# Norm factors of a hybrid encoder layer: one product with ones, a root on ScalarE and a Newton step on VectorE in place of column sums, power and broadcast

## The chip, the cores and the metric

The kernel runs on one core of one Trainium2 chip. The metric is the device time in microseconds (us) of one execution, as the median of several runs. The engines are called as the profile calls them: PE is TensorE (its weight loads are PEld), DVE is VectorE, ACT is ScalarE, POOL is GpSimd, SP is SyncE, which here issues most of the loads.

## What is computed

One layer of a hybrid encoder is applied to 1024 prompt frames and 64 sample frames (1088 positions in all, 1024 channels). Every norm divides by the root of a mean square over channels:

```python
def rmsnorm(x, g):
    y = xf * lax.rsqrt(jnp.mean(xf * xf, axis=-1, keepdims=True) + EPS) * g

def layer(x, ...):
    hn = rmsnorm(x, g_pre1);  z = hn @ w_in            # gate_a | xa | u | v
    h = rg_lru(causal_dwconv(xa, ...), ...)
    ya = rmsnorm(h * gelu(gate_a), g_out_a)            # half 0 of the output norm
    yb = rmsnorm(spatial_gate(u, layernorm(v), w_s), g_out_b)   # half 1
    mix = concatenate([ya, yb]) @ w_o
    x = x + rmsnorm(mix, g_post1)                      # rr1 below
    up = rmsnorm(x, g_pre2) @ w_up                     # rr2 below
    f = (gelu(conv(up)[:D_FF]) * conv(up)[D_FF:]) @ w_down
    x = x + rmsnorm(f, g_post2)                        # finish below
```

EPS is 1e-6. The change concerns how `rsqrt(mean + EPS)`, the norm factor of each position, is made and brought to all 128 partitions.

## The kernel before

Channels lie on the 128 partitions and positions along the columns, so a sum over channels is a sum over partitions, which PE makes. `cs(c)` cuts the 1088 columns in three chunks (364, 364, 360), `qs(q)` in four quarters (274, 274, 274, 266). Matrix products are made from operands split in a high and a low part (`split`, L139 to L142: ACT rounds the high part, DVE subtracts for the low one), three products each.

A norm factor is made in two steps. `rstd_head` (L187) lets PE sum the squares: three blocks of up to 95 columns are loaded as weights and multiplied with a single column of ones (L193, six instructions, since an fp32 product is issued in two), so that the sums of a block stand on its partitions, in three columns. `rstd_small` scales and adds EPS on DVE (L184) and raises to the power -0.5 on POOL (L185). `rstd_tail` (L200) brings the factors to all partitions with three products of the broadcast factors with the identity (L205, six instructions) and copies the result out of PSUM on ACT (L209). There are 20 such factors:

- half 1 of the output norm, four quarters (`y_split(c, 1)`), stepped through while the gate tiles 0 to 2 run on PE (`gate_tile`, products L425, evacuation by DVE in L551, gelu on ACT L553, product with h L555). The normed rows are made on DVE in L605 and split in L607;
- half 0, four quarters (`y_split(c, 0)`);
- `post1` (L701), twice a quarter c: the post-norm (rr1, applied in L711, residual added in L712, stored in L716) and the pre-norm (rr2, applied in L737), then the split into the operands bh and bl and, after each second quarter, differences of operands (L750). While the quarters c = 2 and 3 go through this, PE already makes the first up-projection products of the quarters 0 to 2 (`pre_up`, L775, three quarters c in a row);
- `finish` for three column ranges (272, 272, 284) of the down-projection's output, applied in L1112 eight times each, beside the last products (L1067), whose weights DVE combines in L1007 and splits in L142;
- `finish_last` for the last 260 columns, at the end.

The Tile framework schedules: each engine executes its instructions in a fixed order, found from the order of the program and from priorities (`tc.high_priority(offset=PRI)` pulls instructions ahead). The pool `stp` has 2 PSUM buffers, which the sums, the broadcasts and the gates of the recurrence share; `mmp` has the other 6, so that two gate tiles of three chunks fill it. The order of SP's queue is that of the program: the store L716 stands ahead of the loads of w_up.

Of the kernel before, what the change touches and what calls it, by code (L numbers as in the profile page):

```python
# [14 lines left out]
P = 128  # L15
# [52 lines left out]
def layer_kernel(ctx: ExitStack, tc, xT, w_fm, w_v, w_o, w_up, w_down, w_g, w_s, par, bc, yT, small, vn_out):  # L68
# [14 lines left out]
    def big_tile(dt=F32, shape=(P, TW), name="t"):  # L83
        return big.tile(list(shape), dt, tag="t", name=name)

    def tmp_tile(w, name="d"):
        return tmp.tile([P, 288], F32, tag="d", name=name)[:, :w]
# [17 lines left out]
    def qs(q):  # L105
        return slice(q * QW, min(q * QW + QW, T))
# [28 lines left out]
    nc.gpsimd.memset(ones, 1.0)  # L135
    mhalf = const.tile([P, 16], F32, name="mhalf")
    sm = const.tile([P, NSMALL], F32, name="sm")

    def split(hi, lo, src, scale=None):  # L139
        nc.scalar.activation(hi, src, AF.Copy, scale=1.0 if scale is None else scale)  # L140
# [43 lines left out]
            nc.vector.tensor_scalar(v[:n[0], :n[1]], src, 1.0 / dim, EPS, op0=ALU.mult, op1=ALU.add)  # L184
            nc.gpsimd.tensor_tensor(out, v[:n[0], :n[1]], mhalf[:n[0], :n[1]], op=ALU.pow)  # L185

    def rstd_head(ssq, dim, more=None):  # L187
        w = ssq.shape[-1]
        sb = -(-w // NSB)
        st = stp.tile([P, 512], F32, tag="st", name="st")  # L190
        for b in range(NSB):
            o = min(b * sb, w - sb)
            nc.tensor.matmul(st[:sb, b:b + 1], ssq[:, o:o + sb], ones[:, 0:1], start=True, stop=more is None)  # L193
            if more is not None:
                nc.tensor.matmul(st[:sb, b:b + 1], more[:, o:o + sb], ones[:, 0:1], start=False, stop=True)
        rs = tiny.tile([P, 16], F32, tag="rs", name="rs")
        rstd_small(rs[:sb, :NSB], st[:sb, :NSB], (sb, NSB), dim)
        return rs, sb, w

    def rstd_tail(head, out):  # L200
        rs, sb, w = head
        bp = stp.tile([P, 512], F32, tag="st", name="bp")
        for b in range(NSB):
            lo, hi = b * sb, min(b * sb + sb, w)
            mm = nc.tensor.matmul(bp[:, lo:hi], rs[:sb, b:b + 1].to_broadcast([sb, P]), ident[:sb, lo + sb - hi:sb],  # L205
                                  start=True, stop=True)
            if b == 0:
                tc.keep_in_program_order(mm)
        nc.scalar.activation(out, bp[:, :w], AF.Copy)  # L209
        return bp[:, :w]  # L210

    def add_sq(acc, src, first, eng=None):
        if first:
# [379 lines left out]
    yh, yl = {}, {}  # L593

    def y_split(c, half):
        head = rstd_head((sat if half == 0 else sbt)[:, qs(c)], DA, None if half else sat3[c])
        yield
        w = qw(c)
        rr = tmp_tile(w, name="rr")
        rstd_tail(head, rr)  # L600
        th, tl = big_tile(F32R, name="yh"), big_tile(F32R, name="yl")
        for i in range(4):
            k = half * 4 + i
            y = (hst[i] if half == 0 else s[i])[:, qs(c)]
            nc.vector.scalar_tensor_tensor(y, y, pv("g_out", k), rr, op0=ALU.mult, op1=ALU.mult)  # L605
            yh[k, c], yl[k, c] = th[:, fourth(i, w)], tl[:, fourth(i, w)]
            split(yh[k, c], yl[k, c], y)  # L607
            if i == 1:
                yield
# [5 lines left out]
    def run(gen):  # L615
        for _ in gen:
            pass

    ys = [y_split(c, 1) for c in range(4)]

    def y_steps(n):
# [499 lines left out]

    def finish_last(cols, more):
        w = cols.stop - cols.start
        head = rstd_head(ssqt[0][:, cols], D, more)
        scale_f(3, cols)
        rr = tmp_tile(w, name="rrf")
        bp = rstd_tail(head, rr)
        for g, q in ((1, nc.sync), (0, nc.scalar)):
            for m in range(4):
                f = fg[g][:, m, :]  # L1130
                nc.vector.tensor_tensor(f, f, bp, op=ALU.mult)
            nc.gpsimd.dma_start(yT[:, 4 * g:4 * g + 4, cols], fg[g], accum_op=ALU.add)
# [145 lines left out]
```

## Time and profile before

| what | value |
|---|---|
| median of 3 runs | 1176.99 us (1176.88 to 1177.64) |
| profiled execution, its own time | 1176.07 us |
| its span | 1173.9 us |
| mean granted TensorE clock | 0.987 of full |
| busy share: PE, DVE, ACT, POOL | 96%, 72%, 46%, 15% |
| chain that ended last, by engine | PE 86%, issue 6%, DMA 3%, DVE 2%, POOL 1%, ACT 1% |

The span is what the profile's rows cover; the execution's own time is 2.2 us more, and the median of the runs 0.92 us above that. An engine's busy share is an average over the whole span: stages in which DVE is full stand beside others in which it waits. The chain is followed back from the last instruction, at each step to what released it. In a timeline, a row holds one or several like instructions, their start, the time from the first's start to the last's end, and in brackets the idle time ahead of it with what ended it.

### The profile page before, as it was taken

The page shows a single profiled execution, that of the slowest core. Times are in us where ns is not written, and L with a number is a line of the kernel's source. Part 1 is how long each engine was busy: PE and PEld are TensorE (multiplying, and loading weights), DVE is VectorE, ACT ScalarE, POOL GpSimd, SP SyncE. Part 2 cuts the span into 40 slices and gives each one's busy share as a digit, 9 for nine tenths or more (in the row PEclk, how much of TensorE's full clock was granted, in tenths as well). Part 3 has the DMA queues.
Part 4 walks back from the last instruction along what each step waited for, and adds up shares of the span by engine and source line. Part 5 has one row for each costly group of instructions (what it writes and reads, how often), then busy time and mean ns, then how long its engine had stood idle before and what let it go on. Part 6 is the DMA issues. An engine that isn't in the chain of part 4 may idle for free.

```text
span 1173.9 us, 20616 instructions
## 1 busy us (share of the span) xinstructions
PE 1132.0 (96%) x8420; PEld 1109.0 (94%) x8420; DVE 841.0 (72%) x1363; ACT 534.2 (46%) x876; POOL 172.0 (15%) x291
## 2 busy tenths in 40 slices
PE   6899999999998999999999999999999999999984
PEld 4689999999998999999999999999999999999984
DVE  4568585865678789877877787787789365855753
ACT  4521675645444464444444454454456432523331
POOL 1030001110001113220211111112013000001213
PEclk8999999999999999999999999999999999999987
DMA  9811111140224123221322332232256779555925
GB/s 316 211 54 42 36 37 36 37 129 1 78 96 166 41 79 130 103 103 57 129 99 74 107 114 85 80 130 81 69 207 232 282 256 338 180 213 179 274 31 77
DMA packets 51566, 146.38 MB, mean 125 GB/s; under 512 B 5520, under 2 KB 21392, under 8 KB 51376
## 3 DMA queue, kind: packets, MB, share of 16 engines
q1 hardware_dynamic: 35936, 110.66, 27.3%
q0 software_dynamic: 15312, 34.27, 10.4%
q8 instruction: 66, 1.08, 0.4%
q14 instruction: 28, 0.23, 0.1%
q10 hardware_dynamic: 224, 0.14, 0.0%
HBM read 109.34 MB, written 41.99 MB: 129 GB/s over the span
## 4 chain that ended last, share of the span: by engine, by line
PE 86%; issue 6%; DMA 3%; DVE 2%; POOL 1%; ACT 1%; SPq 0%; POOLq 0%; DVEq 0%; ACTq 0%
PE up L906 40%; PE dps L1067 16%; PE ps L425 12%; PE ops L650 7%; PE pps L775 4%; PE vps L290 2%; DMA xr<-in_xT_dram 1%; DMA wraw<-in_w_v_dram 1%; PE gps L511 1%; PE bp L205 1%; POOL out_dram L1113 1%; PE sp L382 1%; PE st L193 1%; DVE gl L142 1%; ACT whi L140 1%
## 5 line engine op out<-in xcount | busy, mean ns | idle before, releaser
L906 PE MATMUL up<-bh,wop 128*128 128x274 f32 x2464 | 472.3, 290 | 0.0
L906 PEld LDWEIGHTS up<-bh,wop 128*128 128x128 f32 x2464 | 389.1, 189 | 1.7 <-ACT uraw L920 0.9
L906 PE MATMUL up<-bl,wop 128*128 128x274 f32 x1232 | 356.4, 289 | 0.0
L906 PEld LDWEIGHTS up<-bl,wop 128*128 128x128 f32 x1232 | 233.4, 189 | 0.0
L1067 PE MATMUL dps<-gh,whi 128*128 128x272 f32 x576 | 119.7, 289 | 0.7 <-ACT whi L140 0.5
L1067 PE MATMUL dps<-gl,whi 128*128 128x272 f32 x576 | 119.6, 288 | 0.0
L1067 PE MATMUL dps<-gh,wlo 128*128 128x272 f32 x576 | 119.1, 288 | 0.1
L142 DVE TENSOR_TENSOR wlo<-wraw,whi 128x1024 fp32r<-128x1024 f32 x70 | 85.4, 1221 | 35.4 <-ACT whi L140 34.8
L140 ACT ACTIVATE whi<-wraw 128x1024 fp32r<-128x1024 f32 x70 | 73.4, 1055 | 73.8 <-DVE wraw L1007 56.9
L140 ACT ACTIVATE wop<-wsum 128x512 fp32r<-128x512 f32 x88 | 53.0, 626 | 107.7 <-DVE wsum L862 105.3
L920 ACT ACTIVATE uraw<-up 128x274 f32<-128x274 f32 x176 | 65.6, 389 | 64.2 <-PE up L906 63.9
L1067 PEld LDWEIGHTS dps<-gh,whi 128*128 128x128 f32 x576 | 90.3, 188 | 1.1 <-ACT whi L140 0.7
L1067 PEld LDWEIGHTS dps<-gh,wlo 128*128 128x128 f32 x576 | 90.2, 188 | 0.4 <-DVE wlo L142 0.3
L1067 PEld LDWEIGHTS dps<-gl,whi 128*128 128x128 f32 x576 | 90.6, 188 | 0.0
L806 DVE SCALAR_TENSOR_TENSOR yg<-uraw,pt,yg 128x1090 f32<-128x1090 f32 (+1 forms) x48 | 64.8, 1350 | 26.2 <-ACT yg L804 26.2
L925 DVE TENSOR_TENSOR uraw<-up,uraw 128x274 f32<-128x274 f32 x132 | 56.3, 438 | 33.5 <-PE up L906 30.6
L650 PE MATMUL ops<-yh,whi 128*128 128x274 f32 (+1 forms) x256 | 75.3, 294 | 0.0
L650 PE MATMUL ops<-yl,whi 128*128 128x274 f32 (+1 forms) x256 | 73.8, 288 | 0.0
L650 PE MATMUL ops<-yh,wlo 128*128 128x274 f32 (+1 forms) x256 | 73.8, 288 | 0.0
L425 PE MATMUL ps<-xh,whi 128*128 128x364 f32 (+3 forms) x296 | 69.5, 328 | 0.0
L806 DVE SCALAR_TENSOR_TENSOR yv<-uraw,pt,yv 128x1090 f32<-128x1090 f32 (+1 forms) x48 | 64.6, 1346 | 4.8 <-ACT yv L804 4.7
L425 PE MATMUL ps<-xh,wlo 128*128 128x364 f32 (+3 forms) x296 | 67.6, 324 | 0.0
(220 smaller groups left out, 2143.7 us busy)
## 6 DMA issues: line engine op xcount, KB each, us to landing
wraw<-in_w_up_dram SPq DMA_DIRECT2D x48, 512.0 KB, 4.1
graw<-bd SPq DMA_DIRECT2D x42, 544.0 KB, 6.4
wraw<-in_w_down_dram SPq DMA_DIRECT2D x42, 512.0 KB, 5.4
bd<-yg POOLq DMA_DIRECT2D x36, 272.0 KB, 3.4
wraw<-sd SPq DMA_DIRECT2D x18, 512.0 KB, 5.4
bd<-ta POOLq DMA_DIRECT2D x24, 272.0 KB, 3.2
bd<-tb POOLq DMA_DIRECT2D x24, 272.0 KB, 3.0
wraw<-in_w_fm_dram SPq DMA_DIRECT2D x12, 512.0 KB, 3.6
```

The costliest lines, as they stand in the source:

```text
L140: nc.scalar.activation(hi, src, AF.Copy, scale=1.0 if scale is None else scale)
L142: nc.vector.tensor_tensor(lo, src, hi.bitcast(F32), op=ALU.subtract)
L193: nc.tensor.matmul(st[:sb, b:b + 1], ssq[:, o:o + sb], ones[:, 0:1], start=True, stop=more is None)
L290: nc.tensor.matmul(ps[b][:vrows(b), :], a[:, vcols(b)], wt[:, o:o + 512], start=False, stop=(k == KD - 1 and q == 2))
L425: nc.tensor.matmul(ps[c], wt[:, k * P:(k + 1) * P], at[k][:, cols], start=(k == 0 and q == 0), stop=(k == KD - 1 and q == 2))
L650: nc.tensor.matmul(ps, wt[:, i * 256 + mi * P:i * 256 + (mi + 1) * P], a[k, c], start=(first and i == 0 and j == 0), stop=(last and i == 3 ...
L775: nc.tensor.matmul(ps, wt[:, k * P:(k + 1) * P], a[k, c], start=(k == 0 and j == 0), stop=(k == KD - 1 and j == 2))
L806: nc.vector.scalar_tensor_tensor(y[:, d:TG], x[:, :TG - d], tap(2 - d), y[:, d:TG], op0=ALU.mult, op1=ALU.add)
L906: nc.tensor.matmul(dst[c], wt[:, k * P:(k + 1) * P], at[:, fourth(k)], start=(start and k == 0 and q == 0), stop=(k == 3 and q == 2), skip ...
L920: nc.scalar.activation(dst[c], src[c], AF.Copy)
L925: nc.vector.tensor_tensor(dst[c], src[c], p[c], op=ALU.add)
L1067: nc.tensor.matmul(ps, wt[:, k * 256 + mi * P:k * 256 + (mi + 1) * P], at[:, o + a:o + b], start=(first and k == 0 and q == 0), stop=(last ...
```

## The change

Fourteen factors are made in a new way, in place of fifteen of the old. PE multiplies the squares with a 128x128 tile of ones (one fp32 product, two instructions over all columns), so that each partition gets every sum at once. ACT takes the root of mean + EPS from PSUM; DVE takes the reciprocal; three DVE instructions make one Newton step with the sum that still stands in PSUM. The power on POOL, the broadcast products and the copy on ACT are gone there. Half 1 of the output norm is made in three chunks instead of four quarters, all of them ahead of the gate tiles. Half 0 and `finish_last` keep the old way under new names.

```diff
+    epst = const.tile([P, 1], F32, name="epst")
+    nc.gpsimd.memset(epst, EPS)
...
-    def rstd_head(ssq, dim, more=None):
+    def pow_head(ssq, dim, more=None):
...
-    def rstd_tail(head, out):
+    def pow_tail(head, out):
...
+    def rstd_head(ssq, dim, more=None):
+        w = ssq.shape[-1]
+        st = stp.tile([P, 512], F32, tag="st", name="sts")[:, :w]
+        nc.tensor.matmul(st, ones, ssq, start=True, stop=more is None)
+        if more is not None:
+            nc.tensor.matmul(st, ones, more, start=False, stop=True)
+        return st, dim
+
+    def rstd_tail(head, out):
+        st, dim = head
+        w = st.shape[-1]
+        e = (big_tile(name="rse") if w > 288 else tmp_tile(w, name="rse"))[:, :w]
+        with tc.high_priority(offset=PRI):
+            nc.scalar.activation(e, st, AF.Sqrt, scale=1.0 / dim, bias=epst)
+            nc.vector.reciprocal(out, e)
+            nc.vector.scalar_tensor_tensor(e, st, EPS * dim, out, op0=ALU.add, op1=ALU.mult)
+            nc.vector.scalar_tensor_tensor(e, e, -0.5 / dim, out, op0=ALU.mult, op1=ALU.mult)
+            nc.vector.scalar_tensor_tensor(out, e, 1.5, out, op0=ALU.add, op1=ALU.mult)
...
     def y_split(c, half):
-        head = rstd_head((sat if half == 0 else sbt)[:, qs(c)], DA, None if half else sat3[c])
-        yield
         w = qw(c)
-        rr = tmp_tile(w, name="rr")
-        rstd_tail(head, rr)
+        if half == 0:
+            head = pow_head(sat[:, qs(c)], DA, sat3[c])
+            yield
+            rr = tmp_tile(w, name="rr")
+            pow_tail(head, rr)
+        else:
+            yield
+            rr = rrb[:, qs(c)]
...
+    rrb = big_tile(name="rrb")[:, :T]
+    for c in range(3):
+        rstd_tail(rstd_head(sbt[:, cs(c)], DA), rrb[:, cs(c)])
     ys = [y_split(c, 1) for c in range(4)]
...
     def finish_last(cols, more):
...
-        head = rstd_head(ssqt[0][:, cols], D, more)
+        head = pow_head(ssqt[0][:, cols], D, more)
...
-        bp = rstd_tail(head, rr)
+        bp = pow_tail(head, rr)
```

In the changed kernel the new instructions are PE's product in the new `rstd_head` (its output is `sts`), the root in L227, the reciprocal in L228 and the Newton step in L229 to L231. Of the lines before, L551 is L572 there, L605 is L630, L142 is L144, L218 is L239, L737 is L765, L1007 is L1035, L1076 is L1104 and L1112 is L1140.

The order of DVE at the first gate tile, before (m and h are the last tile of the recurrence, L532 and L533 its scan; s are the rows of half 1, yl their low parts, gt the gate tile that leaves PSUM):

```order
L525 SCALAR_TENSOR_TENSOR m<-m,r 128x1088
L605 SCALAR_TENSOR_TENSOR s<-s,pt,rr 128x274 x4
L530 TENSOR_TENSOR m<-m,ig 128x1088
L532 SCALAR_TENSOR_TENSOR h<-a,m 128x1024
L533 SCALAR_TENSOR_TENSOR h<-a,pt,m 128x64
L142 TENSOR_TENSOR wlo<-wraw,whi 128x1024
L142 TENSOR_TENSOR yl<-s,yh 128x274 x4
L551 TENSOR_TENSOR gt<-ps,rbt 128x364 x2
L551 TENSOR_TENSOR gt<-ps,rbt 128x360
```

The same place in the changed kernel, from the scan on (rrb is the factor of half 1, rse a scratch tile):

```order
L553 SCALAR_TENSOR_TENSOR h<-a,m 128x1024
L228 RECIPROCAL rrb<-rse 128x364 x2
L229 SCALAR_TENSOR_TENSOR rse<-sts,rrb 128x364 x2
L230 SCALAR_TENSOR_TENSOR rse<-rse,rrb 128x364 x2
L231 SCALAR_TENSOR_TENSOR rrb<-rse,rrb 128x364
L228 RECIPROCAL rrb<-rse 128x360
L231 SCALAR_TENSOR_TENSOR rrb<-rse,rrb 128x364
L229 SCALAR_TENSOR_TENSOR rse<-sts,rrb 128x360
L554 SCALAR_TENSOR_TENSOR h<-a,pt,m 128x64
L230 SCALAR_TENSOR_TENSOR rse<-rse,rrb 128x360
L144 TENSOR_TENSOR wlo<-wraw,whi 128x1024
L231 SCALAR_TENSOR_TENSOR rrb<-rse,rrb 128x360
```

Three reciprocals and nine further instructions now stand between the scan and the first row of half 1 (L630), and with it ahead of the evacuation of gate tile 0 (L572), which stands behind the first four rows. The third sum has no PSUM buffer of `stp` until the first L229 has read its own.

The order of DVE at the third quarter's pre-norm and the fourth's post-norm, before (rr_3607 is rr2 of c = 2; the sum for rr1 of c = 3 goes through L184):

```order
L218 TENSOR_TENSOR ssq_o<-ssq_o,sq 128x266 x2
L737 SCALAR_TENSOR_TENSOR mix<-xs,pt,rr_3607 128x274
L218 TENSOR_TENSOR ssq_o<-ssq_o,sq 128x266
L737 SCALAR_TENSOR_TENSOR mix<-xs,pt,rr_3607 128x274
L184 TENSOR_SCALAR v<-st 89x3
L737 SCALAR_TENSOR_TENSOR mix<-xs,pt,rr_3607 128x274 x6
```

The same place in the changed kernel (rr_3547 is rr2 of c = 2, rr_3628 is rr1 of c = 3):

```order
L228 RECIPROCAL rr_3547<-rse 128x274
L239 TENSOR_TENSOR ssq_o<-ssq_o,sq 128x266
L229 SCALAR_TENSOR_TENSOR rse<-sts,rr_3547 128x274
L230 SCALAR_TENSOR_TENSOR rse<-rse,rr_3547 128x274
L231 SCALAR_TENSOR_TENSOR rr_3547<-rse,rr_3547 128x274
L228 RECIPROCAL rr_3628<-rse 128x266
L765 SCALAR_TENSOR_TENSOR mix<-xs,pt,rr_3547 128x274
L229 SCALAR_TENSOR_TENSOR rse<-sts,rr_3628 128x266
L765 SCALAR_TENSOR_TENSOR mix<-xs,pt,rr_3547 128x274
L230 SCALAR_TENSOR_TENSOR rse<-rse,rr_3628 128x266
L765 SCALAR_TENSOR_TENSOR mix<-xs,pt,rr_3547 128x274
L231 SCALAR_TENSOR_TENSOR rr_3628<-rse,rr_3628 128x266
```

Four instructions stand ahead of the first row of c = 2 (L765), and the four of the next factor between its rows.

The order of DVE at the second of the three `finish` ranges, before (facc is the down-projection's output, wraw a weight that is combined for the next products):

```order
L1112 SCALAR_TENSOR_TENSOR facc<-facc,pt,rrf 128x272
L1076 TENSOR_TENSOR facc<-dps,facc 128x272 x3
L1007 TENSOR_TENSOR wraw<-wraw 128x1024
```

The same place in the changed kernel:

```order
L228 RECIPROCAL rrf<-rse 128x272
L1104 TENSOR_TENSOR facc<-dps,facc 128x272
L229 SCALAR_TENSOR_TENSOR rse<-sts,rrf 128x272
L1104 TENSOR_TENSOR facc<-dps,facc 128x272
L230 SCALAR_TENSOR_TENSOR rse<-rse,rrf 128x272
L1035 TENSOR_TENSOR wraw<-wraw 128x1024
L231 SCALAR_TENSOR_TENSOR rrf<-rse,rrf 128x272
```

The reciprocal and two instructions of the Newton step stand ahead of the combined weight (L1035), and all eight rows of L1140 come together behind it, ahead of the next combined weight.

## Rows read from the trace of the kernel before

**Rows 1.** Page, part 1: busy time, share of the span, instructions.

```profile
PE 1132.0 (96%) x8420; PEld 1109.0 (94%) x8420; DVE 841.0 (72%) x1363; ACT 534.2 (46%) x876; POOL 172.0 (15%) x291
```

**Rows 2.** Stretches: core and stretch, span, busy (instructions) by engine, PEclk, DMA, GB/s.

```profile
216.00:232.00 16.00, 16.00 (x106) 15.99 (x106) 14.11 (x33) 10.45 (x20) 1.89 (x2) 1.00 0.12 38
...
338.00:363.00 25.00, 24.88 (x204) 24.66 (x202) 25.00 (x45) 11.82 (x21) 2.07 (x2) 1.00 0.32 99
363.00:377.30 14.30, 11.41 (x89) 10.98 (x89) 10.07 (x19) 8.87 (x18) 1.92 (x3) 1.00 0.45 169
...
1109.00:1122.00 13.00, 7.55 (x50) 6.52 (x48) 11.88 (x20) 4.90 (x6) 6.19 (x7) 0.90 0.82 145
1122.00:1145.00 23.00, 22.83 (x163) 22.56 (x163) 11.95 (x17) 8.08 (x13) 0.00 (x0) 0.91 0.06 8
```

**Rows 3.** Timeline of PE beside the first gate tile: start, us, engine, line.

```profile
200.95 0.57 PE L193 MATMUL st<-ones,sbt 128*92 128x1 f32 x6
...
201.96 0.57 PE L193 MATMUL st<-ones,sbt 128*92 128x1 f32 x6
...
204.96 0.66 PE L425 MATMUL ps<-xh,wlo 128*128 128x364 f32 x3
205.45 0.80 PE L205 MATMUL bp<-ident,rs 92*128 92x92 f32 x6
...
206.62 0.50 PE L425 MATMUL ps<-xl,whi 128*128 128x364 f32 x2
```

**Rows 4.** Timeline of PE at an fp32 product over 512 columns.

```profile
63.09 1.13 PE L355 MATMUL wsum<-bw,ones 128*128 128x512 f32 x2
...
64.52 0.40 PE L290 MATMUL vps<-wlo,xh 128*128 128x512 f32 x1
64.75 0.40 PE L290 MATMUL vps<-whi,xh 128*128 128x512 f32 x1
```

**Rows 5.** Who waits for POOL's power, over the span: us, times.

```profile
  PE bp L205: 3.6, 4
```

**Rows 6.** L457, L458 and L184 on DVE: ns min/median/max, first and last start, forms.

```profile
L457 DVE RECIPROCAL d<-d x1: 178/178/178, 9.6 to 9.6; 128x4 f32<-128x4 f32 x1
...
L458 DVE TENSOR_TENSOR e<-e,d x1: 161/161/161, 9.8 to 9.8; 128x4 f32<-128x4 f32 x1
...
L184 DVE TENSOR_SCALAR v<-stt x2: 140/153/166, 63.2 to 63.3; 128x8 f32<-128x8 f32 x1, 64x1 f32<-64x1 f32 x1
```

**Rows 7.** Timelines of ACT and DVE at the gate tiles.

```profile
204.21 1.29 DVE L525 SCALAR_TENSOR_TENSOR m<-m,r 128x1088 f32<-128x1088 f32 x1 [1.49 <-ACT m L524]
...
206.71 1.28 ACT L526 ACT_TABLE_LOAD   x1
...
210.69 2.29 DVE L532 TENSOR_TENSOR_SCAN h<-a,m 128x1024 f32<-128x1024 f32 x1
...
237.35 0.98 DVE L551 TENSOR_TENSOR gt<-ps,rbt 128x364 f32<-128x364 f32 x2 [0.73 <-PE ps L425]
```

**Rows 8.** Timelines of SP, ACT and PE at the third and fourth quarter.

```profile
357.31 0.38 SPq L716 DMA_DIRECT2D out_dram<-xs  x1
...
363.39 1.06 ACT L140 ACTIVATE whi<-wraw 128x1024 fp32r<-128x1024 f32 x1 [4.69 <-DMA wraw<-in_w_up_dram]
...
363.87 0.90 PE L205 MATMUL bp<-ident,rs 92*128 92x92 f32 x6 [0.98 <-POOL rs L185]
...
377.31 0.52 PE L775 MATMUL pps<-bh,whi 128*128 128x274 f32 x2 [1.33 <-ACT bh L140]
```

**Rows 9.** Timelines of DVE and PE at the second and third finish.

```profile
1114.80 2.56 DVE L1112 SCALAR_TENSOR_TENSOR facc<-facc,pt,rrf 128x272 f32<-128x272 f32 x6
1117.28 1.22 DVE L1007 TENSOR_TENSOR wraw<-wraw 128x1024 f32<-128x1024 f32 x1
...
1120.64 0.84 PE L1067 MATMUL lps<-gh,whi 128*128 128x284 f32 x2 [4.01 <-ACT gh L140]
...
1147.18 0.91 PE L205 MATMUL bp<-ident,rs 95*128 95x95 f32 x6 [0.62 <-POOL rs L185]
```

## The prediction, made before the changed kernel ran

> **What bounds the kernel now.** I read the page's busy shares first: PE 96%, DVE 72% [rows 1]. On that alone each microsecond taken from PE counts, and work put on DVE is free. The shares are means, so I then cut the span into stretches where the factors are made [rows 2]. Beside the gate tiles (216 to 232) DVE is busy 14.11 of 16 us. At the third quarter (338 to 363) it is busy 25.00 of 25. Around the second finish (1109 to 1122) it is busy 11.88 of 13, and PE only 7.55. In the last two stages the end of the chain is DVE's, and PE waits behind it. The timelines say what ends those waits: PE's product at 377.31 waits 1.33 us for ACT's bh, which DVE's rows feed [rows 8], and the one at 1120.64 waits 4.01 us for gh, which stands behind a weight that DVE combines at 1117.28 [rows 9].
>
> Everything is worked against the profiled execution's own time, 1176.07 us; the median of the runs lies 0.92 above it, and I add that at the end. 0.2% is 2.35 us, about what a measurement of this kernel can tell from no change.
>
> **What PE saves.** Three matmuls over 364 columns take 0.49 us (204.96 to 205.45). Two sums of squares start at 200.95 and 201.96 with one such group between them, so a sum takes 1.01 - 0.49 = 0.52; from 205.45 to 206.62 are one broadcast and one group, so a broadcast takes 0.68 [rows 3]. Fifteen of the twenty factors are removed: 15 x 1.2 = 18 us. The new product is two fp32 instructions over all columns. At 63.09 such a pair over 512 columns and two plain products at the 0.23 of the next ones (64.52 to 64.75) take 1.43 together, so the pair takes 0.97, or 1.89 ns a column [rows 4]. Half 1 has 1088 columns (2.06 us), the eight post1 factors 2176 (4.11), the finishes 828 (1.56): 7.7 us. PE gains **10.3 us** of work. Beside that it waits 3.6 us for POOL's power, four times, [rows 5]; three of the four go (0.98 and 0.62 are two of them [rows 8, 9]), about 2.3 us. If all of it reached the end: -12.6.
>
> **What DVE gets.** A Newton instruction over 272 columns is like one of L1112, six of which take 2.56: 0.42 each [rows 9]. The reciprocal is the price that the trace hardly shows: one instruction over 4 columns, 178 ns, where a two-operand one over 4 columns takes 161 [rows 6]. That operation over 1024 columns takes 1.22 us [rows 9], so 1.04 ns a column and 157 fixed. If the reciprocal has about the same fixed part, 155, its column costs 23/4 = **5.75 ns**. From above: the cheapest row of DVE, 140 ns for one column [rows 6], as its fixed part leaves 38/4 = 9.5 ns. From below: a column is as cheap as any other, 1.04, and the 17 ns more are fixed. I take 5.75, since the row right behind the reciprocal, of the same shape, is its nearest neighbour; the ends stay for the range. 274 columns then cost 0.155 + 1.575 = 1.73; with three Newton instructions (1.26) a factor puts **3.0 us** on DVE where L184 put 0.15. ACT changes little: a root for a copy, and three table loads of 1.28 [rows 7], in stretches where ACT waits for others; POOL loses 15 powers that nobody else waits for.
>
> **The gate tiles.** The scan starts at 210.69 behind four rows of half 1 (4 x 0.42) and a root on ACT that stands behind a copy and a table load (206.71) [rows 7]. Those rows now stand behind it, so it ends near 210.4 rather than 213.0. Then two reciprocals over 364 columns (2 x 2.25 with the fixed part) end at 214.9; the first Newton instruction frees a PSUM buffer at 215.4; only then PE can make the third sum, ACT its root (done 217.6), and the third reciprocal ends at 219.9. The rest of the factor, a weight split, four rows and three low parts (some 6.3 us) stand ahead of gate tile 0's evacuation, which falls to 226 to 228; before, it was served long ahead of need. The third gate tile wants those banks: 24 groups of 0.5 are 12 us, and its evacuation at 237.35 waits for PE [rows 7], so it starts at about 225, less the time that PE has saved by then: 224.3. It stands about 3.4 us. PE saves 4 x 1.18 - 2.06 = 2.66 here: **+0.7**.
>
> **Quarters 0 and 1.** Three of their four factors come where PE has other products: 1.18 - 0.52 = 0.66 saved for each, **-2.0**; the fourth, rr2 of c = 1, falls into DVE's full stretch and costs 0.2, counted below.
>
> **Quarters 2 and 3.** rr1 of c = 2 puts 3.0 us into the stretch in which DVE never rests [rows 2]. Everything behind it shifts by that: the last rows of c = 2, so the store L716 at 357.31, so the loads of w_up that stand behind it in SP's queue, for which ACT waits 4.69 us at 363.39 [rows 8]. Then rr2 of c = 2 and rr1 of c = 3 stand ahead of and between the rows that make bh. The two put 6.0 us on DVE there and take a broadcast and a copy out of the way; DVE is busy only 10.07 of 14.30 in this stretch [rows 2], so some of it fills waits; I take 2.8 as left on the way to bh. PE's product at 377.31, which already waits for bh, so comes 0.2 + 3.0 + 2.8 = **+6.0** later against all that is ahead of it. PE stands 14.30 - 11.41 = 2.9 us in this stretch before [rows 2]; it will stand about 9. What such a pause does to the clock I read at the finish: in a stretch where PE is busy 7.55 of 13 the granted clock falls to 0.90, and it is 0.91 in the 23 us behind it [rows 2]. The levels are 1.2 and 2.4 GHz, so 0.09 missing of 23 us is 2.1 us of work lost. I take **+2.0**. The last factor, rr2 of c = 3, saves 0.7. Sum: 6.0 + 2.0 - 0.7 = **+7.3**. The up-projection is untouched.
>
> **The finishes.** The first and second sit beside PE's products: -0.66 each. At the second, reciprocal and Newton step stand ahead of L1007, and two more rows of L1112 between: 3.0 + 2 x 0.42, and some 0.3 by which the rows of L1112 start later, make the next L1007 come at about 1121.4, where it came at 1117.28 [rows 9], so PE's wait of 4.01 grows by **+4.1**. The third saves 0.66 and the POOL wait of 0.62 [rows 9]. Sum: 4.1 - 2.6 = **+1.5**.
>
> Total: 0.7 - 2.0 + 7.3 + 1.5 = **+7.5**, 1183.6 against the profiled execution, 1184.5 against the median; I write **1184**.
>
> **The rivals.** One number decides most: each further nanosecond a column lengthens four reciprocals of about 270 columns (rr1 and rr2 of c = 2, rr1 of c = 3, the second finish) and three chunks of 364 that stand in a chain, about 2.2 us, and 2.5 with the pause of PE that grows.
>
> *A cheap reciprocal* (1.04 to 2.5 ns). For it: a 4-column row cannot tell a fixed part from a slope. Then the sum falls by 3.3 to 4.7 x 2.5, to about zero or a little below, 1174 to 1180, and the gate tile no longer stalls.
>
> *A dear reciprocal* (8 to 9.5 ns), the fixed part being 140 to 146 as in the cheapest row [rows 6]. The sum is 7.5 + 2.25 x 2.5 = 13.1 at 8 ns and 16.9 at 9.5: 1187 to 1194, centre 1191. The Trainium skill, "VectorE: DVE Perf Modes", Walkthrough, "First, the fixed hardware budget", says that the reciprocal is an iterative divide with a repeat count of 8. If that means eight cycles a column, this rival is the one it names; the sum by the page is the +13 of this rival, by the neighbouring row the +7.5; the row of 178 ns fits the page only with a fixed part below its neighbour's, and no row shows a long reciprocal.
>
> *PE's sum counts in full.* DVE's chains have slack that I don't see (its fixed order can fill waits for DMA and for ACT), and all of -12.6 reaches the end: 1163.5, 1164.4 against the median; half of it 1171. For it: PE is busy 96% [rows 1], and 86% of the chain that ended last is PE's. Against: DVE 25.00 of 25 [rows 2]. It decides if rr1 of c = 2 does not move the store at 357.31.
>
> **Chances.** My forecast 0.45 (1180 to 1188), the dear reciprocal 0.20, the cheap one 0.20, PE's sum 0.15. Faster by over 0.2% (below 1174.6): PE's sum and a quarter of the cheap case, 0.20. Within 0.2%: the rest of the cheap case, 0.15. Slower: 0.65. The range 1172 to 1194 leaves out PE's sum in full and the far end of the dear case; the likeliest case alone is 1180 to 1188.
>
> **What would show it.** In the changed profile: RECIPROCAL over 274 columns at 1.5 to 1.8 us (near 0.45 the cheap case, above 2.1 the dear one); PE's busy time down by about 10; gate tile 0 evacuated after 225, with a PE wait on it of 2 to 5 us; the w_up loads about 3 us later, and PE's wait for bh at the third quarter up from 1.33 to several us, with a granted clock below 1.00 behind it; PE's wait for gh after the second finish near 8 us. I am wrong if the time is below 1176 with the reciprocal at 1.5 us or more: then DVE's chains were not what PE waited for.

## The result

| | before | changed |
|---|---|---|
| median of 4 runs | 1177.32 us (1176.88 to 1177.76) | 1189.64 us (1189.05 to 1189.83) |
| ratio of the times | 1 | 1.0104 (95% interval 1.0086 to 1.0121) |
| profiled execution, its own time | 1176.07 us | 1189.76 us |
| its span | 1173.9 us | 1188.0 us |
| mean granted clock | 0.987 | 0.975 |

The changed kernel is 12.3 us slower. 1184 was forecast with a range of 1172 to 1194: the sign and the range held, the size was 7.5 where 12.3 came.

The page of the changed kernel, part 1 and the chain by engine; they answer to [rows 1] and to the last line of the table before:

```profile
PE 1131.6 (95%) x8268; PEld 1104.7 (93%) x8268; DVE 881.2 (74%) x1404; ACT 539.0 (45%) x878; POOL 157.0 (13%) x277
...
PE 81%; DVE 10%; DMA 4%; issue 2%; ACT 2%; POOL 1%; SPq 0%; POOLq 0%; DVEq 0%; ACTq 0%
```

PE has 152 instructions less and is busy for as long as before, since part of its work ran at the lower clock (in e6 below, with the same 8268 instructions and a mean clock of 0.986, it is busy for 1122.6 us). DVE has 40 us more and now holds 10% of the chain, where it had 2%.

Where the time went is read from the first and last start of PE's products, stage by stage. Before (line, tile, count, ns min/median/max, first and last start):

```profile
L425 PE MATMUL ps<-xh,whi x296: 283/328/433, 80.6 to 249.2; 128*128 128x364 f32 x88, 128*128 128x360 f32 x44, 128*128 128x274 f32 x12, 128*128 128x266 f32 x4
...
L650 PE MATMUL ops<-yh,whi x256: 279/289/374, 250.5 to 358.7; 128*128 128x274 f32 x96, 128*128 128x266 f32 x32
...
L775 PE MATMUL pps<-bh,whi x128: 284/290/395, 359.0 to 414.8; 128*128 128x274 f32 x128
```

The changed kernel, the same products:

```profile
L446 PE MATMUL ps<-xh,whi x296: 283/328/644, 81.4 to 252.1; 128*128 128x364 f32 x88, 128*128 128x360 f32 x44, 128*128 128x274 f32 x12, 128*128 128x266 f32 x4
...
L678 PE MATMUL ops<-yh,whi x256: 280/289/493, 252.5 to 359.9; 128*128 128x274 f32 x96, 128*128 128x266 f32 x32
...
L803 PE MATMUL pps<-bh,whi x128: 283/290/817, 360.3 to 425.0; 128*128 128x274 f32 x128
```

With the products `up`, `dps` and `lps` read in the same way, each stage from its first product to the next stage's first (us):

| stage | before | changed | difference | forecast |
|---|---|---|---|---|
| gate tiles and all before (from the first ps) | 169.9 | 171.1 | +1.2 | +0.7 |
| output projection, quarters 0 and 1 beside it (ops) | 108.5 | 107.8 | -0.7 | -2.0 |
| first up products, quarters 2 and 3 (pps) | 56.2 | 65.1 | +8.9 | +7.3 |
| up-projection | 472.7 | 472.7 | 0 | 0 |
| down products, first finish (dps) | 220.8 | 219.2 | -1.6 | -0.7 |
| last products, second and third finish (lps, to the last one) | 47.6 | 51.1 | +3.5 | +2.2 |
| the end behind them | 17.6 | 19.6 | +2.0 | 0 |

That makes 13.3 us, and 0.8 by which the first product started later: 14.1, the difference of the spans. It is more than the 12.3 of the medians because each kernel gives one execution here. How far one execution can be trusted, the runs below tell: the first product starts anywhere from 79.1 to 84.2 us in them, and in e1, e3 and e7, whose edits do not touch the stage of the first up products, that stage takes 58.8, 57.6 and 56.1 us. Differences of a stage below some 3 us are therefore taken as shown only where a wait or several runs say the same.

The price on which the forecast turned, reciprocals by shape:

```profile
L228 DVE RECIPROCAL rr<-rse x8: 1817/1858/1868, 296.6 to 399.6; 128x274 f32<-128x274 f32 x6, 128x266 f32<-128x266 f32 x2
L228 DVE RECIPROCAL rrb<-rse x3: 2369/2402/2403, 211.1 to 218.1; 128x364 f32<-128x364 f32 x2, 128x360 f32<-128x360 f32 x1
```

Against the 178 ns for four columns [rows 6], 274 columns at 1858 are 6.2 ns a column with a fixed part of 153. The forecast had 5.75 and 155. The Trainium skill, "VectorE: DVE Perf Modes", Walkthrough, "First, the fixed hardware budget", gives the reciprocal a repeat count of 8. The rival that stood beside it had 8 to 9.5 ns a column; these rows lie below it, at six times the 1.04 ns of a two-operand column, not eight.

The gate tiles in the changed kernel, DVE, ACT and PE:

```profile
211.13 4.69 DVE L228 RECIPROCAL rrb<-rse 128x364 f32<-128x364 f32 x2
...
218.15 2.40 DVE L228 RECIPROCAL rrb<-rse 128x360 f32<-128x360 f32 x1 [0.16 <-ACT rse L227]
...
226.28 0.97 DVE L572 TENSOR_TENSOR gt<-ps,rbt 128x364 f32<-128x364 f32 x2
...
217.55 0.56 ACT L227 ACTIVATE rse<-sts,epst 128x360 f32<-128x360 f32 x1 [9.31 <-PE sts L217]
...
226.96 1.02 PE L446 MATMUL ps<-xh,whi 128*128 128x364 f32 x2 [3.48 <-ACT yh L142]
```

The third root waits 9.3 us for its sum, which has no PSUM buffer until the first Newton instruction; the evacuation of gate tile 0 falls to 226.28 and the third gate tile waits 3.48 us. The bracket names ACT's yh, which ends at 226.83; the product does not read it, but by the kernel's buffers it writes a bank that the evacuation of 226.28 has to free first. The forecast had 226 to 228 and 3.4.

The quarters 2 and 3 in the changed kernel, DVE, SP, ACT and PE, beside [rows 8]:

```profile
348.34 1.86 DVE L228 RECIPROCAL rr<-rse 128x274 f32<-128x274 f32 x1
...
355.09 0.91 DVE L739 SCALAR_TENSOR_TENSOR mix<-mix,pt,rr 128x274 f32<-128x274 f32 x2
...
363.96 1.50 SPq L168 DMA_DIRECT2D wraw<-in_w_up_dram  x2
...
369.05 1.06 ACT L142 ACTIVATE whi<-wraw 128x1024 fp32r<-128x1024 f32 x1 [4.13 <-DMA wraw<-in_w_up_dram]
...
364.98 0.60 PE L803 MATMUL pps<-bh,wlo 128*128 128x274 f32 x1 [4.31 <-DVE wlo L144]
...
386.35 1.05 PE L803 MATMUL pps<-bh,whi 128*128 128x274 f32 x3 [5.66 <-ACT bh L142]
```

The same rows and loads before:

```profile
348.07 0.91 DVE L711 SCALAR_TENSOR_TENSOR mix<-mix,pt,rr 128x274 f32<-128x274 f32 x2
...
357.79 1.49 SPq L166 DMA_DIRECT2D wraw<-in_w_up_dram  x2
```

The rows of rr1 of c = 2 start 7.0 us later, and the two loads of w_up that stand behind their store are issued 6.2 later, where about 3 were expected. PE stands twice, 4.31 us for a weight's low part, which the forecast did not have, and 5.66 for bh, where it stood 1.33. Only the second wait reached the end. The chain that ended last has no work of PE between 336.24 and 386.35; it goes through DVE's rows, the loads of w_up and ACT's bh (start, us, what):

```profile
340.88 2.97 DVE mix L765 x7
...
364.50 6.64 DMA wraw<-in_w_up_dram
...
386.35 12.12 PE pps L803 x79
```

A faster PE ahead of 386.35 would only have waited longer there. So the stage is cut at that product, which stood at 377.31 before. From the stage's first product to it are 26.05 us, before 18.3: +7.7, where the forecast had +6.0. From it to the end of the stage are 39.05, before 37.9: +1.2, where the forecast had 2.0 for the clock less 0.7. The granted clock over this second part is 0.95 (before 1.00), which on 39.05 us is about 1.9 of PE's time.

PE's own account of the whole stage, from its first to its last product (columns as in [rows 2]); before, changed, and the run e6 below, in which DVE has no part in the new factors:

```profile
359.00:415.10 56.10, 53.09 (x422) 52.43 (x421) 45.23 (x83) 25.94 (x49) 8.33 (x12) 1.00 0.30 102
```
```profile
360.20:425.20 65.00, 54.94 (x391) 53.68 (x390) 59.88 (x105) 30.03 (x56) 3.71 (x8) 0.89 0.29 97
```
```profile
352.80:404.80 52.00, 50.29 (x391) 49.71 (x390) 45.69 (x82) 28.10 (x52) 2.87 (x8) 1.00 0.30 102
```

Idle PE rose from 3.01 to 10.06 us. The 391 instructions that take 50.29 at the full clock in e6 take 54.94 here at a mean of 0.89, so PE lost 4.6 us of work to the clock. Of that, 2.7 (the 4.6 less the 1.9 above; the clock is 0.81 ahead of 386.35) lie ahead of the wait of 5.66 and cost the kernel nothing.

The second finish in the changed kernel, DVE and PE, beside [rows 9]:

```profile
1130.42 1.22 DVE L1035 TENSOR_TENSOR wraw<-wraw 128x1024 f32<-128x1024 f32 x1
...
1124.25 0.60 PE L1095 MATMUL lps<-gh,whi 128*128 128x284 f32 x1 [3.67 <-ACT whi L142]
...
1133.79 0.53 PE L1095 MATMUL lps<-gh,whi 128*128 128x284 f32 x2 [2.96 <-ACT gh L142]
```

The combined weight behind the eight rows starts 13.1 us after the first of the last products (1117.3), where it started 8.6 after it before (1117.28 against 1108.7).

### The profile page after: what moved, and what is told of

Its sections match the earlier page's. It is cut to its first block, busy times and chain, and to the rows that moved or that the text cites. A ratio compares the mean times of both kernels' runs of the same rounds, so it can differ in the third digit from the quotient of the medians.

```text
span 1188.0 us, 20331 instructions
## 1 busy us (share of the span) xinstructions
PE 1131.6 (95%) x8268; PEld 1104.7 (93%) x8268; DVE 881.2 (74%) x1404; ACT 539.0 (45%) x878; POOL 157.0 (13%) x277
## 3 DMA queue, kind: packets, MB, share of 16 engines
q0 software_dynamic: 15312, 34.27, 10.3%
## 4 chain that ended last, share of the span: by engine, by line
PE 81%; DVE 10%; DMA 4%; issue 2%; ACT 2%; POOL 1%; SPq 0%; POOLq 0%; DVEq 0%; ACTq 0%
PE up L934 40%; PE dps L1095 16%; PE ps L446 11%; PE pps L803 3%; PE ops L678 3%; PE vps L311 2%; PE lps L1095 2%; DMA xr<-in_xT_dram 1%; DMA wraw<-in_w_v_dram 1%; PE gps L532 1%; DVE rr L228 1%; DVE mix L739 1%; ACT whi L142 1%; PE sp L403 1%; DVE mix L765 1%
## 5 line engine op out<-in xcount | busy, mean ns | idle before, releaser
L144 DVE TENSOR_TENSOR wlo<-wraw,whi 128x1024 fp32r<-128x1024 f32 x70 | 85.3, 1220 | 34.7 <-ACT whi L142 34.6
L142 ACT ACTIVATE whi<-wraw 128x1024 fp32r<-128x1024 f32 x70 | 73.4, 1055 | 75.7 <-DVE wraw L1035 58.2
L142 ACT ACTIVATE wop<-wsum 128x512 fp32r<-128x512 f32 x88 | 53.1, 627 | 108.4 <-DVE wsum L890 106.5
L948 ACT ACTIVATE uraw<-up 128x274 f32<-128x274 f32 x176 | 65.8, 390 | 65.2 <-PE up L934 64.8
```

What stands on the lines that cost most here:

```text
L144: nc.vector.tensor_tensor(lo, src, hi.bitcast(F32), op=ALU.subtract)
L948: nc.scalar.activation(dst[c], src[c], AF.Copy)
```

## The experiments

Each kernel is the changed one with an edit; its median was set against runs of the kernel before on the same chip, and the difference below is the ratio times 1177. Stages and rows come from one profiled execution of each. In e4 the factors are a constant, in e6 they are the root and not its inverse: these two leave out what the layer needs and are there for their time alone.

| run | new factors | ratio to before (95%) | difference, us |
|---|---|---|---|
| e1 | half 1 only | 1.0027 (1.0005 to 1.0048) | +3.2 |
| e2 | post1 only | 1.0056 (1.0034 to 1.0079) | +6.6 |
| e3 | finish only | 1.0026 (1.0009 to 1.0044) | +3.1 |
| e4 | all, reciprocal replaced | 0.9982 (0.9962 to 1.0002) | -2.1 |
| e5 | all, no Newton step | 1.0002 (0.9990 to 1.0014) | +0.2 |
| e6 | all, nothing on DVE | 0.9907 (0.9892 to 0.9921) | -10.9 |
| e7 | third finish only | 1.0016 (1.0006 to 1.0025) | +1.9 |
| e8 | post1 of the quarters 2, 3 | 1.0084 (1.0067 to 1.0100) | +9.9 |
| e9 | rr1 of quarter 2 only | 1.0070 (1.0043 to 1.0098) | +8.2 |
| e10 | some, no Newton step | 0.9996 (0.9978 to 1.0014) | -0.5 |
| e11 | all, by logarithm on ACT | 1.0032 (1.0019 to 1.0045) | +3.8 |
| e12 | as e9, issued close together | 1.0040 (1.0028 to 1.0052) | +4.7 |

**e1 to e3: one group of factors at a time.** The other factors call the old functions (here for post1 in e1 and e3):

```diff
-        head = rstd_head(ssq, D)
+        head = pow_head(ssq, D)
...
-        rstd_tail(head, rr)
+        pow_tail(head, rr)
```

> Only the four factors of half 1 are made the new way (three chunks); post1 and finish keep the old way. Theory (each group of factors costs what its own stage shows): PE saves 2.7 us of work and stands about 3.5 us for the gate tile's banks, so 1177.3 + 0.7 to 1.3, that is 1177.5 to 1179; PE's wait at the third gate tile is there as in the changed kernel. Rival (the late rows of half 1 push a backlog down DVE's queue, which is what the quarters pay for): 1181 or more, with DVE fuller between 300 and 345 us than the 27.8 us of before.

> Only the eight factors of post1 are made the new way. Theory: +8 us against before (1184 to 1187): the stretch of quarters 2 and 3 loses 9 as in the changed kernel, the early quarters gain 0.8. Rival of the backlog from half 1: rr2 of the second quarter then has its room on DVE again and costs next to nothing, so 3 us less, +5 (1182). Rival that PE's work decides: -5 (1172).

> Only the three finish factors are made the new way. Theory: +3.9 us (1180 to 1182): 1.8 until the last product of the down-projection, with PE's waits after the second finish grown from 4.0 to about 7.5, and 2.1 at the end, where POOL's last power starts only when POOL has issued the eight transfers of the third finish. Rival (the end of the kernel is late only because all before it is): 1.8 at most, 1179, and the last wait for POOL stays at 1.3 us.

The three add to +12.9, so within their intervals (2 to 3 us each way) the groups cost what they cost alone.

In e1 the gate stage takes 171.1 us as in the changed kernel, with PE's wait of 3.48 there. By its time alone e1 decides nothing: +3.2 lies above the theory's 0.7 to 1.3 and just below the +3.7 of its rival, and the interval (0.6 to 5.7) holds both. What decides is DVE: between 300 and 345 us it is as full as before, 27.77 against 27.78, and 27.77 again in the stretch moved by the 4.8 us by which this execution runs later, so half 1 pushes no backlog that far. The profiled execution is the longest of e1's ten. In its pps stage PE's waits are those of before (0.87, 0.70 and 1.32 us for 0.98, 0.70 and 1.33), and yet the clock is 0.53 from 385 to 390, right behind the last of them, where before it stayed at 1.00; the stage is 2.6 us longer.

e2 speaks against the backlog too: its pps stage lasts 65.5 us, the 65.1 of the changed kernel, and half 1 is not in it; its time of +6.6 (4.0 to 9.3) holds the theory's 8 and that rival's 5. Its output projection gains 2.2, the forecast's 2.0, of which the changed kernel kept 0.7.

In e3 the down products are 1.4 shorter, the lps stage 3.1 longer and the end 1.8 longer, with the last broadcast waiting 2.63 us for POOL. The changed kernel's end, and then the end before:

```profile
1166.09 6.24 POOL L1141 DMA_DIRECT2D out_dram<-facc  x7 [0.19 <-DVE facc L1140]
1170.89 2.36 POOL L187 TENSOR_TENSOR rs<-v,mhalf 87x3 f32<-87x3 f32 x1
...
1173.31 1.58 PE L207 MATMUL bp<-ident,rs 87*128 87x87 f32 x6 [2.69 <-POOL rs L187]
```
```profile
1158.93 0.87 POOL L185 TENSOR_TENSOR rs<-v,mhalf 87x3 f32<-87x3 f32 x1 [2.24 <-DVE v L184]
1159.86 1.07 PE L205 MATMUL bp<-ident,rs 87*128 87x87 f32 x6 [1.28 <-POOL rs L185]
```

The third finish's transfers are issued by POOL, and POOL also makes the last power. It took 0.87 us before, when the transfers were through; here its row begins at 1170.89 and ends at 1173.25, 0.9 behind the end of the last of them (1172.33). The wait is 1.4 longer, and the broadcast takes 0.5 more.

**e4 and e5: the reciprocal, and the Newton step.** The edit of e4; e5 leaves out L229 to L231:

```diff
-            nc.vector.reciprocal(out, e)
+            nc.vector.tensor_tensor(out, e, e, op=ALU.is_equal)
-            nc.vector.scalar_tensor_tensor(e, e, -0.5 / dim, out, op0=ALU.mult, op1=ALU.mult)
+            nc.vector.scalar_tensor_tensor(e, e, 0.0, out, op0=ALU.mult, op1=ALU.mult)
```

> The changed kernel with every long reciprocal replaced by a two-operand instruction of the same shape that gives 1, and the second Newton constant set to 0, so the factors are a constant 1.5; all else is the same. Theory (the price of the reciprocal's columns decides, 2.5 us for each ns a column): the instruction falls from 1.86 to about 0.44 us, 5.2 ns a column, so about 13 us, to 1176 to 1178. Rival (the number of instructions in the chain decides, the three Newton instructions as much as the reciprocal): about half of the loss stays, 1182 to 1184. Rival that PE's work decides once DVE is out of the way: 1168.

> The changed kernel without the Newton step: L229 to L231 are left out, the factor is the plain reciprocal of ScalarE's root. DVE keeps 1.86 us a factor and loses 1.3. Theory (DVE's time decides, whatever instruction it goes to): 1.3 us a factor off gives about what the cheap reciprocal gave (1.42 us off, 12 to 14 us), so 1176 to 1180 against 1177 to 1178.6 of before. Rival (it is the reciprocal as such, which stands ahead of what it feeds): 1185 to 1188.

Both kernels come down to the time of before: 1177.39 and 1177.50. e4 takes 1.4 us off DVE for each factor and e5 1.3, the one by the reciprocal, the other by the three instructions behind it. It is DVE's time that counts, not the reciprocal as such; nor is it the number of dependent instructions, four in e4 and one in e5. For the last 1.3 or 1.4 us that every factor puts on DVE, the kernel pays 9 to 10 for each microsecond. With e6 as the other end (below), the first 1.7 to 1.9 cost 5 to 6 each: the price rises with what DVE already carries.

**e6: nothing on DVE.**

```diff
-            nc.scalar.activation(e, st, AF.Sqrt, scale=1.0 / dim, bias=epst)
-            nc.vector.reciprocal(out, e)
...
+            nc.scalar.activation(out, st, AF.Sqrt, scale=1.0 / dim, bias=epst)
```

> All of the new factor's work on DVE is left out: ScalarE's root is written as the factor itself, so rows are multiplied by the root of the mean square and not by its inverse; PE's products, ScalarE's instruction and the tables stay. Theory: PE's savings then reach the end, except where PE already waited: 1165 to 1169, with 3.5 to 4 us gained at the gate tiles. Rival (the stretch of quarters 2 and 3 waits for loads and ScalarE as much as for DVE): 1170 to 1174.

1165.59 us, in the theory's range and below the rival's: the saving that the change makes on PE is there, 10.9 us by the ratio. The gate stage gains 3.0, somewhat less than expected. The forecast's PE sum of -12.6 was nearly right as a sum; it is DVE that gave it back.

**e7: the third finish alone.**

> Only the third finish factor is made the new way. Theory of the end (rows 3 us late put POOL's eight transfer issues late, and the last power waits behind them): 1.3 us saved before the last product, 1.4 to 2 lost behind it, so within 1 us of before, and in the trace the wait of the last broadcast for POOL at 2.6 us in place of 1.3. Rival (the second finish's delay does it): that wait stays at 1.3 and the kernel is 1 us faster.

The lps stage is 1.6 us shorter and the end 2.8 longer, with the power behind the seven transfers that end at 1160.6:

```profile
1154.39 6.24 POOL L1136 DMA_DIRECT2D out_dram<-facc  x7 [0.20 <-DVE facc L1135]
1158.22 3.31 POOL L187 TENSOR_TENSOR rs<-v,mhalf 87x3 f32<-87x3 f32 x1
...
1161.59 1.58 PE L207 MATMUL bp<-ident,rs 87*128 87x87 f32 x6 [3.65 <-POOL rs L187]
```

The wait is 3.65, where 2.6 was expected, so the third factor alone does it; the loss of 1.9 us by the median (0.7 to 2.9) is larger than the theory had.

**e8: the quarters 2 and 3 alone.**

> Only the four post1 factors of the quarters 2 and 3 are made the new way. Theory (the new factors of the quarters 0 and 1 use up the idle time that DVE has before the third quarter, so that rr2 of the second comes 3 us late): without them the stretch of the first up-projection products lasts 6 us longer than before, not 9.4, and the kernel is 5.5 to 6.5 slower. Rival (the loss is made by the quarters 2 and 3 alone): 9 us slower.

The rival was right: 9.9 us slower, and a pps stage of 66.0. Yet rr2 of c = 1 does start its rows on time here, at 338.76 (337.91 before, and this execution's first product is 0.9 later too). So something else had to put c = 2 late, and one factor was tried by itself.

**e9: one factor, rr1 of c = 2.**

> One single factor is made the new way: rr1 of the third quarter, the first of post1 there. Theory as first put (it costs its own 3 us on DVE, since DVE never rests there): the rows L733 start 3 to 3.5 us later, 1179.5 to 1180.5. Rival (the fixed order spreads its Newton step among the subtractions, a low part and a weight split that stood behind those rows before, so the rows, the store and the loads of w_up behind it wait for these too): L733 starts about 7.5 us later than L711 did (348.07), and the kernel is 5 to 6 us slower, 1182 to 1183.

+8.2 us (5.1 to 11.5) for a factor whose own instructions take 3.2; the rival had the rows right and 5 to 6 us for the time. DVE, from the reciprocal to the rows:

```profile
348.13 1.86 DVE L228 RECIPROCAL rr<-rse 128x274 f32<-128x274 f32 x1
349.90 1.23 DVE L144 TENSOR_TENSOR bl<-mix,bh 128x1096 fp32r<-128x1096 f32 x1
351.06 0.43 DVE L229 SCALAR_TENSOR_TENSOR rse<-sts,rr 128x274 f32<-128x274 f32 x1
351.40 1.29 DVE L772 TENSOR_TENSOR mix<-mix 128x1096 f32<-128x1096 f32 x1
352.61 0.44 DVE L230 SCALAR_TENSOR_TENSOR rse<-rse,rr 128x274 f32<-128x274 f32 x1
352.96 1.29 DVE L772 TENSOR_TENSOR mix<-mix 128x1096 f32<-128x1096 f32 x1
354.18 0.44 DVE L231 SCALAR_TENSOR_TENSOR rr<-rse,rr 128x274 f32<-128x274 f32 x1
354.53 1.22 DVE L144 TENSOR_TENSOR wlo<-wraw,whi 128x1024 fp32r<-128x1024 f32 x1
355.67 0.91 DVE L733 SCALAR_TENSOR_TENSOR mix<-mix,pt,rr 128x274 f32<-128x274 f32 x2
```

Each of the four waits on the one ahead, and the fixed order puts a long instruction of other work into each gap, four of some 1.2 us, which before stood behind the rows. They are not lost work; but the rows start 7.6 us late, and with them the store and the loads of w_up. PE waits 3.66 us for wlo and then runs at the lower clock:

```profile
365.56 0.60 PE L797 MATMUL pps<-bh,wlo 128*128 128x274 f32 x1 [3.66 <-DVE wlo L144]
365.95 0.43 PE L797 MATMUL pps<-bh,whi 128*128 128x274 f32 x1
366.18 0.43 PE L797 MATMUL pps<-bl,whi 128*128 128x274 f32 x1
...
375.16 0.29 PE L797 MATMUL pps<-bh,whi 128*128 128x274 f32 x1
375.29 0.29 PE L797 MATMUL pps<-bl,whi 128*128 128x274 f32 x1
```

From 365.95 to 366.18 is 0.23 us a product, from 375.16 to 375.29 it is 0.13; the granted clock from 365.5 to 375.2 is 0.50, the level of 1.2 GHz. In these 9.4 us PE also waits 1.11 for POOL, so some 8.3 us of work went at half speed, 3.6 more than at the full clock. Not all of that counts. The stage is 65.8 us long, 9.6 longer than before, made of three parts (rounded): 6.3 until POOL's power for rr2 of c = 2 starts (367.73, 9.3 us into the stage; before 361.97, 3.0 into it), 1.7 from there to bh's product (384.77), and 1.5 behind that, where the clock is 0.96. About 3 of the 9.6 are thus the clock's.

**e12: the same factor, with the gaps closed.**

```diff
+    def behind():
+        return tc.issue_after(held[0].ins) if held else nullcontext()
...
-        split(hi, lo, src)
+        with behind():
+            split(hi, lo, src)
```

`held` keeps the last Newton instruction; the subtractions L750 stand behind it in the same way.

> As the run with rr1 of the third quarter alone, and the subtractions and splits of the second quarter's operands that are traced behind this factor are issued behind its last Newton instruction, so that reciprocal and Newton step stand together on DVE; what is computed is the same. Theory (more than half of that factor's 7.8 us was what stood in the gaps of its Newton step): the rows L739 start about 3.2 us later than L711 did (351.3 in place of 348.07, and of 355.67 with the gaps filled), PE's wait for the weight's low part shrinks from 3.7 us or goes, and the kernel is 2 to 4 us slower than before, 1180 to 1181. Rival (a factor that is 3 us late already brings PE's pause and its lower clock): 1184 to 1186.

DVE and PE in e12 (line numbers 2 to 7 higher):

```profile
347.07 1.87 DVE L230 RECIPROCAL rr<-rse 128x274 f32<-128x274 f32 x1 [0.46 <-ACT rse L229]
...
350.29 1.29 DVE L779 TENSOR_TENSOR mix<-mix 128x1096 f32<-128x1096 f32 x1
351.50 0.92 DVE L739 SCALAR_TENSOR_TENSOR mix<-mix,pt,rr 128x274 f32<-128x274 f32 x2
...
362.26 0.60 PE L804 MATMUL pps<-bh,wlo 128*128 128x274 f32 x1 [3.89 <-DVE wlo L144]
```

The rows start at 351.50, 3.4 us late and as expected, 4.2 earlier than in e9. But PE's wait for wlo stays, 3.89 us, since that split still stands behind the rows, and the granted clock in 360 to 375 is 0.66 as in e9. The kernel is 4.7 us slower than before, between the theory's 2 to 4 and the rival's 7 to 9. Of the 4.2 us by which the rows come earlier, the stage keeps 0.9 in the profiled executions (64.9 for 65.8). The intervals of e9 and e12 overlap: how much of the 8.2 the gaps make is left open; by the one trace of each it is the smaller part. That 3.4 us of lateness with PE's pause and its clock is enough for about 5 is shown.

**e10 and e11: other ways to keep PE's saving.** e10 is without the Newton step and takes the new way only for half 1, c = 0, rr1 of c = 1 and the first finish:

```diff
-        head = rstd_head(ssq, D)
+        new1, new2 = c in (0, 1), c in (0,)
+        head = rstd_head(ssq, D) if new1 else pow_head(ssq, D)
```

> The new way only where DVE has room or where PE's banks wait, and without the Newton step: half 1, both factors of the first quarter, rr1 of the second, the first finish; all others the old way. Theory (PE's savings reach the end where DVE is not the last to arrive): 3.7 us at the gate tiles, about 2 at the early quarters, 0.7 to 1.5 at the first finish, so 1170 to 1172 against 1177.3. Rival (the early quarters' factors use up the idle time of DVE that the third quarter lives on): 1174 to 1177.

No gain by the median: 1178.76 against 1178.1. In its profiled execution the gate stage is 3.8 us shorter, as expected (no wait for the banks), and the output projection 3.1 longer: PE between 250 and 300 us is busy 48.65 of 50 at a granted clock of 0.97, waiting 1.35 us for POOL at 254.52. The pps stage is 2.7 longer too, with the waits of before and a clock of 0.94, as in e1. The rival's outcome, though by another place than it named; the cause behind the wait at 254.52 was not tried.

e11 leaves DVE out and stays on ACT:

```diff
-            nc.scalar.activation(e, st, AF.Sqrt, scale=1.0 / dim, bias=epst)
...
+            nc.scalar.activation(out, st, AF.Ln, scale=1.0 / dim, bias=epst)
+            nc.scalar.activation(out, out, AF.Exp, scale=-0.5)
```

> The fourteen factors are made on ScalarE alone: logarithm of mean + EPS from PSUM, then the exponential of -0.5 times it; no reciprocal and no Newton step. ScalarE gets two instructions and, as a rule, two table loads of 1.28 us for each factor, 3.5 us in all; DVE gets nothing. Theory (it was DVE's time that ate PE's saving): ScalarE is busy 46% and takes it at a small cost, 1166 to 1170. Rival (any engine that puts 3.5 us in these chains costs the same): 1180 to 1190.

+3.8 us (2.2 to 5.3): not the theory's gain; 1181.34 lies at the lower end of the rival's 1180 to 1190. The gate stage is 2.9 shorter and the pps stage 2.6, but the output projection is 10.2 longer, where this row of the waits of PE stands first:

```profile
PE sts L217 <- DVE ss L235: 9.4, 3, 4.5
```

Three sums of squares come late, 9.4 us in all: in 286 to 350 us DVE's rows wait 5.6 and 6.2 us (L735 and L761, twice each) for the factor from ACT, whose 3.5 us with its table loads are now in the chain, and the squares are made of those rows. An engine that is busy 46% on the whole is not free in the stage that matters, ACT as little as DVE. None but e6, which leaves DVE's part out, is clearly faster than the kernel before.

## Why the prediction was right, and where its sizes were off

- **PE's saving**: 10.3 us of work and 2.3 of POOL waits forecast. In e6 PE is busy 9.4 us less than before (1122.6 for 1132.0), and the kernel is 10.9 faster of the 12.6. Right as a sum; in the changed kernel itself the mark "PE's busy time down by about 10" is not met (1131.6), as the lower clock took it.
- **DVE's 3 us a factor** at 5.75 ns a column: 3.2 at 6.2. Right, and with e4 to e6 DVE's time is shown to be the cause, in instructions of either kind. That 5.75 came so near was partly luck: as the prediction says, a row of four columns cannot tell a fixed part from a slope.
- **The gate tiles**: evacuation at 226.28 and a wait of 3.48 for 226 to 228 and 3.4; the stage +1.2 for +0.7.
- **Quarters 0 and 1**: -2.0 held with post1 alone (e2: -2.2); beside half 1 only -0.7 was left, and e1's execution has the stage 1.6 longer. Why was not tried.
- **Quarters 2 and 3**, +8.9 for +7.3. The term that was too small is the "+6.0" by which PE's product for bh comes later; it measured 7.7. It rests on "rr1 of c = 2 puts 3.0 us into the stretch in which DVE never rests" and "Everything behind it shifts by that". The rows of rr1 came 7.0 later and the loads of w_up 6.2. Its own instructions were counted and not what the fixed order puts between them: in e9 the rows are 7.6 late for 3.2 of work. The "+2.0" for the clock fits: 1.9 behind that product. That PE would also wait for a weight's low part was not seen; in the changed kernel the later wait for bh covers it, in e9 and e12 it counts.
- **The finishes**: forecast +1.5, measured +1.9 (-1.6 and +3.5). The weight L1035 comes 4.5 later in its stage for +4.1. PE's two waits there are 3.67 and 2.96 us, 6.6 for the 8 that were named as the mark; the rest of the lateness is work at a lower clock (0.87 over the stage, 0.93 before).
- **The end**: nothing was forecast, and +2.0 came. The step "The third saves 0.66 and the POOL wait of 0.62" left out that POOL's queue holds the third finish's transfers ahead of the last power (e3, e7).

By its time alone 1189.64 lies outside the likeliest 1180 to 1188 and inside the dear reciprocal's 1187 to 1194. That rival fell with the 6.2 ns: a reciprocal over 274 columns takes 1.86 us, just above the mark of 1.5 to 1.8 and below the 2.1 of the dear case, and the missing 5 us are those of the other terms above. The cheap one fell with the same row; its "1174 to 1180" was too high for its own sum, which takes 8 to 12 off the 7.5 and so gives 1173 to 1176. PE's sum as a rival fell with e4 to e6: it comes true only when DVE's share is taken away.

## What to carry to other kernels

Time a chain of dependent instructions by what the schedule puts between them, not by their own length: on a full engine with a fixed order, four short steps with 3.2 us of work held their rows up for 7.6. How much of such lateness the kernel pays is another question, and is settled at the wait that ends last: with the gaps closed the rows came 4.2 us sooner and the stage was 0.9 shorter. Work that is taken from the busiest engine is worth nothing where another engine's chain arrives last. There a wait of the busiest engine can cost more than its length, through the clock behind it, but only as far as no later wait covers the lost time. Before moving a step off an engine that looks idle, look at that engine's queue at the place, issues of transfers included.

## What the runs showed of the hardware that was not expected

- PE's pace behind a pause: after 3.66 us without work in e9, products at 0.23 us each in place of 0.13 for 9.4 us, and a granted clock of 0.66 over 360 to 375, where the kernel before, with waits of up to 1.33 us in this stage, kept 1.00.
- The same short waits do not always leave the clock alone: 0.98, 0.70 and 1.33 us (or within 0.1 of that) were followed by 1.00 in the kernel before and in e7, by 0.75 from 377 to 382 in e3 and by 0.53 from 385 to 390 in e1, which makes this stage 1.4 and 2.6 us longer with no other difference in PE's waits. What decides between them no run here shows.
- A reciprocal over 274 columns takes 1.86 us, over 364 columns 2.40, so 6.2 ns a column, about six times a two-operand instruction's 1.04.
- A table load on ACT of 1.28 us came with 13 of the 14 logarithms and again with 13 of the 14 exponentials (e11), so two instructions of 0.49 and 0.43 us cost 3.5.
- A power on POOL that takes 0.87 us by itself ended 2.4 us after its start in the changed kernel and 3.3 in e7, each time 0.9 behind the end of the transfers that POOL was issuing.
